# Turning softmax probabilities as rounded-kind data after a copy inside SBUF, in a one-core hybrid encoder layer

## The chip, the core and the metric

The program runs on one core of a Trainium2 chip. The metric is the device time of one execution in microseconds (us); the lower the better. Five engines work side by side, each through its own instruction stream in order: TensorE (PE, with a separate record PEld for the loading of the stationary operand), VectorE (DVE), ScalarE (ACT), GpSimd (POOL) and SyncE (SP). In this kernel SP issues nearly all DMA transfers. A stream that waits for a semaphore holds up everything behind it on the same engine.

## The reference

One encoder layer is applied to two token groups (1024 and 256 rows of width 2048, here 10 tiles of 128 rows). Everything is fp32. Cut to the lines that matter here:

```
hn = rms_norm(x, norm_g);  proj = hn @ w_in               # 2048 -> 4896 columns
o_ssd = chunked two-way state-space scan over xbc, dt     # 16 heads
# window attention, 8 heads of 64, 2 key heads, |t-s| <= 128, sink logit:
s = q @ k.T * 64**-0.5 - slope * dist                     # masked to the band
m = max(max(s), sink);  pr = exp(s - m)
probs = pr / (sum(pr) + exp(sink - m));  o_att = (probs @ v) * silu(z_att)
# memory attention, 4 heads of 128 against 256 memory rows:
pm = softmax(mq @ mk.T * 128**-0.5);  o_mem = (pm @ mv) * silu(z_mem)
y = x + concat[o_ssd, o_att, o_mem] @ w_out
```

For `probs @ v` and `pm @ mv` the tensor engine contracts over the partition axis, so the probabilities, which come out with queries on partitions, have to be turned to have keys on partitions.

## The kernel before, in words

The large products (`x @ w_in`, `mem @ w_mem_kv`, `o @ w_out`) are the trunk. Each weight block is loaded by SP into a `wraw` tile (pool of `RB = 4`), split by ACT and DVE into a high and a low part of the rounded fp32 kind (`wsplit`, L202 and L203, `fp32r`, pools of 3), and multiplied in three passes (L254 to L256 for token tiles, L289 to L291 for feature tiles, L1199 to L1201 for the seven-product blocks). The fp32r kind streams a 512-column product in about 0.23 us on this core; a plain fp32 product of the same width shows as two records of about 0.43 us each.

Beside the trunk run two lanes, which are queues of Python generators. Lane 0 holds `k_prep`, `attn` and `mem_attn`, tile after tile; lane 1 holds the state-space work `ssd_up` and `ssd_down`. After each step of a trunk block `run` calls `pump(rates)`: each lane is owed its rate (a number of generator steps; `RATES` has one pair, lane 0 and lane 1, for each weight block of each of the two row groups), and each step owed runs the generator to its next `yield`. So a `yield` is a unit of distance, and the rate says how many such units go to one trunk step.

The program is written in a tile framework. What the Python emits is a list in priority order; a planner then lays it out, engine by engine, with its own durations: at each point an engine takes the earliest instruction of the list whose inputs the planner holds to be ready and whose buffers are free. Slots of a pool tag are given out when the first writer of a tile is placed. The order that results is fixed in the program; on the chip each engine follows it and waits where an input is late.

`attn(t)` (one tile of 128 queries) loads `q`, normalises it, turns it in two halves (`pq`, L616, as fp32r with the fp32r identity `identr`), and loads the gate `za`. Then it goes over four head pairs `rr`: `scores(rr)` makes two score products into PSUM (`psc`, L632 and L633), DVE adds the distance bias into `lg` (L634, pool of 2), reduces the maximum, ACT takes the exponentials (L647), DVE scales by the reciprocal sum (L652, tile `lg<-lg,den`). `turn_(rr)` turns the probabilities as plain fp32 with `ident` (`ppt`, L664: two key heads times 2 or 3 blocks of 128) and ACT copies them out (`pT`, L665). `values(half)` multiplies two turned head pairs with `v` (`po`, L674) and DVE applies the gate into `oT` (L677). `mem_attn(t)` does the same over two head pairs `hp` with four blocks each: `pms` (L737 to L739), `mpr` (L746, L751), `pmt` (L759, fp32, `ident`), `mpT` (L763), `pmo` (L774).

The tag `wa` (pool of `WA = 5` slots of 128x512 fp32) holds `q`, its squares, the split `qh`, `za`/`zm`, `oT`/`moT` and small helpers of the lane. The functions that the change touches, with their lines:

Of the kernel before, what the change touches and what calls it, by code (L numbers as in the profile page):

```python
# [10 lines left out]
F32 = mybir.dt.float32  # L11
F32R = mybir.dt.float32r
# [7 lines left out]
P = 128  # L20
# [8 lines left out]
CH, WB, RB, WA, WBB = 4, 3, 4, 5, 4  # L29
RBB = 3  # L30

RATES = ({'kv': (2.0, 1.0), 'mq': (2.4, 1.6), 'z0': (2.2, 1.7), 'z1': (2.2, 1.7)},
         {'kv': (1.2, 1.5), 'x': (1.75, 1.85), 'q': (1.6, 2.5), 'za': (1.6, 2.5), 'z0': (1.55, 2.6),
          'z1': (1.55, 2.65), 'mq': (1.55, 2.8), 'zm': (1.55, 2.85), 'o': (1.95, 1.9)})
NEG = -1e30

UNITS = (0, 4, 1, 5, 2, 6, 7, 3, 8, 9)
# [6 lines left out]
def hymba_encoder_kernel(  # L44
# [42 lines left out]
    ident = identr.bitcast(F32)  # L87
# [495 lines left out]
    def attn(t):  # L583
        lo, hi = (0, NS) if t < NS else (NS, NT)
        k0, k1 = max(lo, t - 1), min(hi, t + 2)
        na = k1 - k0
        nk = na * P
        d0 = (k0 - (t - 1)) * P
        s0 = k0 if t < 4 else k0 - 3
        grp, ti = divmod(t, 5)  # L590
        tc_ = slice(ti * P, (ti + 1) * P)
        q = w2("q")
        S.dma_start(q, q_d[t])
        yield
        sq = w2("sq")
        A.activation(sq, q, AF.Square)
        ss = sm.tile([P, 8], F32, tag="s8", name="qss", bufs=4)
        V.reduce_sum(out=ss, in_=hv(sq), axis=AX.X)  # L598
        r = sm.tile([P, 8], F32, tag="s8", name="qr", bufs=4)
        rsqrt(r, ss, 1.0 / 64, 8)  # L600
        for _ in range(3):
            yield
        q3 = hv(q)
        V.tensor_mul(q3, q3, hb(r, 8, 64))
        yield
        qT = []
        for b in range(2):
            qh = mp.tile([P, 4, 2, 64], F32R, tag="wa", name="qh", bufs=WA)
            qb = q3[:, 4 * b:4 * b + 4, :]
            A.activation(qh[:, :, 0, :], qb, AF.Copy)  # L610
            V.tensor_sub(qh[:, :, 1, :], qb, qh[:, :, 0, :].bitcast(F32))
            yield
            ps = psum("pq")
            qf = qh.rearrange("p a b d -> p (a b d)")
            for a in range(4):
                T.transpose(ps[:, a * P:(a + 1) * P].bitcast(F32R), qf[:, a * P:(a + 1) * P], identr)  # L616
            o = mp.tile([P, 512], F32R, tag="qT", name="qT", bufs=2)
            A.activation(o, ps, AF.Copy)
            qT.append(o)
        z = w2("za")  # L620
        S.dma_start(hv(z, 4), zT_d[0][grp][:, :, tc_])
        yield
        sk8 = sinkb.rearrange("p (v r) -> p r v", v=2)
        state_ = {}

        def scores(rr):
            lg = mp.tile([P, 2, 384], F32, tag="lg", name="lg", bufs=2)
            for kv in range(2):
                h = 4 * kv + rr
                ps = psum("psc")  # L630
                st = qT[kv][:, rr * P:(rr + 1) * P]
                T.matmul(ps[:, :nk], st, kT[:, kv, s0 * P:s0 * P + nk], start=True, stop=False)  # L632
                T.matmul(ps[:, :nk], st, kL[:, kv, s0 * P:s0 * P + nk], start=False, stop=True)  # L633
                V.scalar_tensor_tensor(out=lg[:, kv, :nk], in0=ndist[:, d0:d0 + nk], scalar=2.0 ** -(h + 1),  # L634
                                       in1=ps[:, :nk], op0=ALU.mult, op1=ALU.add)
            m = sm.tile([P, 2], F32, tag="m2", name="m", bufs=10)
            V.reduce_max(out=m, in_=lg[:, :, :nk], axis=AX.X)
            sk = sk8[:, rr, :]
            nm = sm.tile([P, 2], F32, tag="m2", name="nm", bufs=10)
            V.tensor_max(m, m, sk)  # L640
            V.tensor_scalar(out=nm, in0=m, scalar1=-1.0, scalar2=None, op0=ALU.mult)
            es = sm.tile([P, 2], F32, tag="m2", name="es", bufs=10)
            V.tensor_add(es, sk, nm)
            A.activation(es, es, AF.Exp)
            den = sm.tile([P, 2], F32, tag="m2", name="den", bufs=10)
            for kv in range(2):
                A.activation(lg[:, kv, :nk], lg[:, kv, :nk], AF.Exp, bias=nm[:, kv:kv + 1],  # L647
                             accum_out=den[:, kv:kv + 1])
            V.tensor_add(den, den, es)
            V.reciprocal(out=den, in_=den)  # L650
            for kv in range(2):
                V.tensor_scalar(out=lg[:, kv, :nk], in0=lg[:, kv, :nk], scalar1=den[:, kv:kv + 1], scalar2=0.5,  # L652
                                op0=ALU.mult, op1=ALU.mult)
            state_[rr] = lg

        def turn_(rr):
            lg = state_.pop(rr)
            if rr % 2 == 0:
                state_["pT"] = mp.tile([P, 2, 2, 384], F32, tag="pT", name="pT", bufs=1)
            pT = state_["pT"]  # L660
            for kv in range(2):
                pt = psum("ppt")
                for a in range(na):
                    T.transpose(pt[:, a * P:(a + 1) * P], lg[:, kv, a * P:(a + 1) * P], ident)  # L664
                A.activation(pT[:, kv, rr % 2, :nk], pt[:, :nk], AF.Copy)  # L665

        oT = w2("oT")

        def values(half):
            pT = state_.pop("pT")  # L670
            po = psum("po")
            for a in range(na):
                for kv in range(2):
                    T.matmul(hv(po[kv * 64:kv * 64 + 64, :2 * P], 2), v_all[:, s0 + a, kv * 64:kv * 64 + 64],  # L674
                             pT[:, kv, :, a * P:(a + 1) * P], start=(a == 0), stop=(a == na - 1))
            c = slice(half * 2 * P, (half + 1) * 2 * P)
            V.tensor_mul(oT[:, c], po[:, :2 * P], z[:, c])  # L677

        scores(0)
        yield  # L680
        scores(1)
        yield
        yield
        turn_(0)
        yield
        scores(2)
        yield
        turn_(1)
        yield
        scores(3)  # L690
        yield
        values(0)
        yield
        turn_(2)
        yield
        turn_(3)
        yield
        yield
        values(1)
        yield  # L700
        S.dma_start(oT_d[0][grp][:, :, tc_], hv(oT, 4))


    def mem_attn(t):
# [26 lines left out]
        def scores(hp):  # L731
            ps = psum("pms")
            for j in range(2):
                h = 2 * hp + j
                c = slice(h * P, (h + 1) * P)
                o = ps[:, j * 256:(j + 1) * 256]
                T.matmul(o, qh[:, c], mkH[:, h, :], start=True, stop=False)  # L737
                T.matmul(o, qh[:, c], mkL[:, h, :], start=False, stop=False)
                T.matmul(o, ql[:, c], mkH[:, h, :], start=False, stop=True)  # L739
            m = sm.tile([P, 2], F32, tag="m2", name="mm", bufs=10)  # L740
            V.reduce_max(out=m, in_=hv(ps, 2), axis=AX.X)
            V.scalar_tensor_tensor(out=m, in0=m, scalar=-1.0, in1=r[:, 2 * hp:2 * hp + 2], op0=ALU.mult, op1=ALU.mult)
            pr = mp.tile([P, 512], F32, tag="lg", name="mpr", bufs=2)
            den = sm.tile([P, 2], F32, tag="m2", name="mden", bufs=10)
            for j in range(2):
                A.activation(pr[:, j * 256:(j + 1) * 256], ps[:, j * 256:(j + 1) * 256], AF.Exp,  # L746
                             scale=r[:, 2 * hp + j:2 * hp + j + 1], bias=m[:, j:j + 1], accum_out=den[:, j:j + 1])
            V.reciprocal(out=den, in_=den)
            for j in range(2):
                c = slice(j * 256, (j + 1) * 256)  # L750
                V.tensor_scalar(out=pr[:, c], in0=pr[:, c], scalar1=den[:, j:j + 1], scalar2=0.5,  # L751
                                op0=ALU.mult, op1=ALU.mult)
            st_[hp] = pr

        def turn_(hp):
            pr = st_[hp]
            pt = psum("pmt")
            for a in range(4):
                T.transpose(pt[:, a * P:(a + 1) * P], pr[:, a * P:(a + 1) * P], ident)  # L759
            if hp == 0:  # L760
                st_["pT"] = mp.tile([P, 2, 768], F32, tag="pT", name="mpT", bufs=1)
            pT = st_["pT"][:, hp, :512]
            A.activation(pT, pt, AF.Copy)  # L763
            st_[hp] = pT
# [13 lines left out]

        scores(0)
        yield  # L780
        scores(1)
        yield
        yield
        turn_(0)
        yield
        turn_(1)
        yield
        values(0)
        yield
        values(1)  # L790
        S.dma_start(oT_d[1][grp][:, :, tc_], hv(oT, 4))
# [889 lines left out]
```

## Time and profile before

| | |
|---|---|
| device time, median of 3 runs | 1804.51 us (1804.37 to 1805.38) |
| profiled execution, first to last instruction (span) | 1800.7 us |
| what the median has beyond that span | 3.8 us |
| PE busy | 1791.2 us, 99% of the span |
| DVE / ACT / POOL busy | 1244.3 / 903.0 / 439.5 us |
| granted TensorE clock | 1.000 over the span |
| DMA packets' share of the 16 engines | 52.7% |

The profile gives no separate device time for the profiled execution beside its span; the three runs agree within 1.0 us, and what lies around the span is taken to be the same in each. Durations of PE records overlap, because matmuls are pipelined: what a matmul costs is the distance from its start to the start of the next, not its recorded length. Waits name the engine and the tile that ended them.

### The profile page before, as it was taken

To read this page: it belongs to the slowest core of one execution; us is meant where nothing else is said; L and a number is where in the kernel's file an instruction comes from. 1 tells how busy PE (TensorE), PEld (TensorE's weight loads), DVE (VectorE), ACT (ScalarE), POOL (GpSimd) and SP (SyncE) were. 2 spreads that over 40 slices of the span, in tenths; PEclk is the share of its full clock that TensorE was granted. 3 is DMA by queue.
4 is the path that set the end of the run, shared out by engine and by line. 5 is a ranking of instruction groups with operands and counts; after the bars stand their busy time and mean duration, and the time that the engine had idled before them with its cause. 6 is when DMAs were issued, how large, how long until landed. Compare 5 with 4: busy or idle time off the path is not lost.

```text
span 1800.7 us, 30423 instructions
## 1 busy us (share of the span) xinstructions
PE 1791.2 (99%) x10546; PEld 1606.1 (89%) x10546; DVE 1244.3 (69%) x2422; ACT 903.0 (50%) x2039; POOL 439.5 (24%) x714
## 2 busy tenths in 40 slices
PE   9999999999999999999999999999999999999999
PEld 7789999999887899999989987887898888889999
DVE  5595788877657978775755866666885654866665
ACT  6554455444445756564435646544574533543332
POOL 0105789961110000000000000001100000058775
PEclk9999999999999999999999999999999999999999
DMA  8664455446544644444436355457785564644442
GB/s 291 198 179 120 138 153 146 129 136 218 164 136 147 184 134 140 121 132 134 119 96 192 110 161 180 128 178 235 231 266 168 184 190 138 216 153 147 142 143 80
DMA packets 198891, 290.58 MB, mean 161 GB/s; under 512 B 18960, under 2 KB 80464, under 8 KB 198736
## 3 DMA queue, kind: packets, MB, share of 16 engines
q1 hardware_dynamic: 198592, 288.57, 52.7%
q8 instruction: 83, 1.36, 0.3%
q14 instruction: 72, 0.59, 0.1%
q10 hardware_dynamic: 144, 0.06, 0.0%
HBM read 231.12 MB, written 57.44 MB: 160 GB/s over the span
## 4 chain that ended last, share of the span: by engine, by line
PE 61%; DVE 1%; ACT 1%; issue 1%; DMA 1%; POOL 0%; POOLq 0%; ACTq 0%; DVEq 0%
PE acc L254 9%; PE acc L256 8%; PE acc L255 8%; PE acc L289 5%; PE acc L291 5%; PE acc L290 5%; PE acc L1199 3%; PE acc L1201 3%; PE acc L1200 3%; PE py L931 2%; PE po L674 1%; PE ppt L664 1%; PE accm L1200 1%; PE accm L1201 1%; PE accm L1199 1%
## 5 line engine op out<-in xcount | busy, mean ns | idle before, releaser
L203 DVE TENSOR_TENSOR wl<-wraw,wh 128x512 fp32r<-128x512 f32 (+1 forms) x480 | 338.9, 708 | 241.3 <-ACT wh L202 230.7
L254 PE MATMUL acc<-wh,xH 128*128 128x512 f32 (+1 forms) x1248 | 481.9, 386 | 0.2 <-ACT mkr L416 0.2
L255 PE MATMUL acc<-wl,xH 128*128 128x512 f32 (+1 forms) x1248 | 472.2, 378 | 0.9 <-DVE wl L203 0.6
L256 PE MATMUL acc<-wh,xL 128*128 128x512 f32 (+1 forms) x1248 | 472.8, 379 | 0.0
L202 ACT ACTIVATE wh<-wraw 128x512 fp32r<-128x512 f32 (+1 forms) x480 | 292.4, 613 | 323.5 <-PE acc L256 173.3
L254 PEld LDWEIGHTS acc<-wh,xH 128*128 128x128 f32 x1248 | 234.5, 188 | 45.1 <-issue 4.8
L255 PEld LDWEIGHTS acc<-wl,xH 128*128 128x128 f32 x1248 | 234.7, 188 | 43.8 <-DVE wl L203 3.3
L256 PEld LDWEIGHTS acc<-wh,xL 128*128 128x128 f32 x1248 | 234.2, 188 | 43.9 <-issue 0.9
L289 PE MATMUL acc<-xH,wh 128*128 128x320 f32 x640 | 204.5, 320 | 0.0
L291 PE MATMUL acc<-xH,wl 128*128 128x320 f32 x640 | 198.6, 310 | 0.0
L290 PE MATMUL acc<-xL,wh 128*128 128x320 f32 x640 | 198.3, 310 | 0.0
L203 DVE TENSOR_TENSOR sl<-ws,sh 128x384 fp32r<-128x384 f32 x144 | 99.6, 695 | 96.9 <-ACT sh L202 96.6
L202 ACT ACTIVATE sh<-ws 128x384 fp32r<-128x384 f32 x144 | 74.6, 523 | 176.5 <-POOL ws L1171 81.5
L1171 POOL TENSOR_TENSOR ws<-wraw 128x128 f32<-128x128 f32 x144 | 91.1, 633 | 202.0 <-DMA wraw<-in_w_in_pairs_dram 83.6
L289 PEld LDWEIGHTS acc<-xH,wh 128*128 128x128 f32 x640 | 120.3, 188 | 4.1 <-issue 3.7
L290 PEld LDWEIGHTS acc<-xL,wh 128*128 128x128 f32 x640 | 120.3, 188 | 2.6 <-issue 2.2
L291 PEld LDWEIGHTS acc<-xH,wl 128*128 128x128 f32 x640 | 120.1, 188 | 0.7 <-issue 0.6
L1171 POOL TENSOR_TENSOR ws<-wraw,ws 128x128 f32<-128x128 f32 x144 | 93.5, 649 | 11.3
L358 DVE SCALAR_TENSOR_TENSOR c<-u,vec,c 128x638 f32<-128x638 f32 (+1 forms) x96 | 88.6, 926 | 10.0 <-ACT c L353 9.7
L1171 POOL TENSOR_TENSOR ws<-ws,wraw 128x128 f32<-128x128 f32 x144 | 94.2, 654 | 0.0
L120 POOL TENSOR_SCALAR qr<-qss 128x8 f32<-128x8 f32 x10 | 4.3, 428 | 366.6 <-DVE qss L598 366.6
L1171 POOL TENSOR_TENSOR wraw<-wraw 128x128 f32<-128x128 f32 x144 | 89.2, 620 | 11.1
(427 smaller groups left out, 3645.1 us busy)
## 6 DMA issues: line engine op xcount, KB each, us to landing
wraw<-in_w_in_laid_dram SPq DMA_DIRECT2D x208, 256.0 KB, 2.8
wraw<-in_w_in_pairs_dram SPq DMA_DIRECT2D x80, 256.0 KB, 2.8
wraw<-in_w_out_laid_dram SPq DMA_DIRECT2D x64, 256.0 KB, 3.5
wraw<-in_w_out_pairs_dram SPq DMA_DIRECT2D x64, 256.0 KB, 2.8
rf<-ac SPq DMA_DIRECT2D x40, 256.0 KB, 3.7
rb<-ac SPq DMA_DIRECT2D x40, 256.0 KB, 4.1
wraw<-in_w_mem_laid_dram SPq DMA_DIRECT2D x32, 256.0 KB, 4.8
xst<-in_x_sample_dram SPq DMA_DIRECT2D x20, 256.0 KB, 4.7
```

The costliest lines, as they stand in the source:

```text
L202: a = A.activation(h, raw, AF.Copy)
L203: b = V.tensor_sub(l, raw, h.bitcast(F32))
L254: T.matmul(ps[t][:, :n], sh, h[:, :n], start=(k_ == 0), stop=False)
L255: T.matmul(ps[t][:, :n], sh, l[:, :n], start=False, stop=False)
L256: T.matmul(ps[t][:, :n], sl, h[:, :n], start=False, stop=(k_ == KT - 1))
L289: T.matmul(o, sh, cur["H", q][:, m, c], start=(k == 0), stop=False)
L290: T.matmul(o, sh, cur["L", q][:, m, c], start=False, stop=False)
L291: T.matmul(o, sl, cur["H", q][:, m, c], start=False, stop=(k == KT - 1))
L358: V.scalar_tensor_tensor(out=c[0], in0=u[:, k:k + n], scalar=cw[k], in1=c[0], op0=ALU.mult, op1=ALU.add)
L1171: G.tensor_tensor(out=o, in0=x, in1=y, op=op)
L1199: T.matmul(ps[p], h, xh, start=(k_ == 0), stop=False)
L1200: T.matmul(ps[p], h, xl, start=False, stop=False)
```

## The change

- In `attn`, each scaled `lg` (two key heads) is copied by two SP transfers from SBUF to SBUF into two new tiles `lgR` of the fp32r kind, 128x384, in the tag `wa`. `turn_` turns `lgR` with `identr`, as fp32r.
- In `mem_attn`, `mpr` is copied by one SP transfer into `mprR` (128x512, fp32r, tag `wa`) and turned in the same way.
- The yields move: `attn` has 12 instead of 11 of them from its first scores to its last values, and four between `scores(rr)` and `turn_(rr)` for every head pair (before three or four). `scores(2)` now follows `turn_(0)` and `scores(3)` follows `turn_(1)` in the same step. `mem_attn` has 8 instead of 6, and four instead of three between the scores and the turn of each head pair; `values(0)` now comes before `turn_(1)`.
- The lane 0 entries of `RATES` are multiplied by about 1.07. Lane 1's are kept.

The transfers copy bits through an fp32 view of the destination; no value is changed by them.

```diff
--- before.py
+++ after.py
@@ -29,9 +29,8 @@
 CH, WB, RB, WA, WBB = 4, 3, 4, 5, 4
 RBB = 3
 
-RATES = ({'kv': (2.0, 1.0), 'mq': (2.4, 1.6), 'z0': (2.2, 1.7), 'z1': (2.2, 1.7)},
-         {'kv': (1.2, 1.5), 'x': (1.75, 1.85), 'q': (1.6, 2.5), 'za': (1.6, 2.5), 'z0': (1.55, 2.6),
-          'z1': (1.55, 2.65), 'mq': (1.55, 2.8), 'zm': (1.55, 2.85), 'o': (1.95, 1.9)})
+RATES = ({'kv': (2.14, 1.0), 'mq': (2.57, 1.6), 'z0': (2.35, 1.7), 'z1': (2.35, 1.7)},
+         {'kv': (1.28, 1.5), 'x': (1.87, 1.85), 'q': (1.71, 2.5), 'za': (1.71, 2.5), 'z0': (1.66, 2.6), 'z1': (1.66, 2.65), 'mq': (1.66, 2.8), 'zm': (1.66, 2.85), 'o': (2.09, 1.9)})
 NEG = -1e30
 
 UNITS = (0, 4, 1, 5, 2, 6, 7, 3, 8, 9)
@@ -651,7 +650,9 @@
             for kv in range(2):
                 V.tensor_scalar(out=lg[:, kv, :nk], in0=lg[:, kv, :nk], scalar1=den[:, kv:kv + 1], scalar2=0.5,
                                 op0=ALU.mult, op1=ALU.mult)
-            state_[rr] = lg
+            state_[rr] = [mp.tile([P, 384], F32R, tag="wa", name="lgR", bufs=WA) for _ in range(2)]
+            for kv in range(2):
+                S.dma_start(state_[rr][kv].bitcast(F32)[:, :nk], lg[:, kv, :nk])
 
         def turn_(rr):
             lg = state_.pop(rr)
@@ -661,7 +662,7 @@
             for kv in range(2):
                 pt = psum("ppt")
                 for a in range(na):
-                    T.transpose(pt[:, a * P:(a + 1) * P], lg[:, kv, a * P:(a + 1) * P], ident)
+                    T.transpose(pt[:, a * P:(a + 1) * P].bitcast(F32R), lg[kv][:, a * P:(a + 1) * P], identr)
                 A.activation(pT[:, kv, rr % 2, :nk], pt[:, :nk], AF.Copy)
 
         oT = w2("oT")
@@ -678,20 +679,21 @@
 
         scores(0)
         yield
+        yield
         scores(1)
         yield
         yield
         turn_(0)
-        yield
         scores(2)
         yield
+        yield
         turn_(1)
-        yield
         scores(3)
         yield
         values(0)
         yield
         turn_(2)
+        yield
         yield
         turn_(3)
         yield
@@ -750,13 +752,14 @@
                 c = slice(j * 256, (j + 1) * 256)
                 V.tensor_scalar(out=pr[:, c], in0=pr[:, c], scalar1=den[:, j:j + 1], scalar2=0.5,
                                 op0=ALU.mult, op1=ALU.mult)
-            st_[hp] = pr
+            st_[hp] = mp.tile([P, 512], F32R, tag="wa", name="mprR", bufs=WA)
+            S.dma_start(st_[hp].bitcast(F32), pr)
 
         def turn_(hp):
             pr = st_[hp]
             pt = psum("pmt")
             for a in range(4):
-                T.transpose(pt[:, a * P:(a + 1) * P], pr[:, a * P:(a + 1) * P], ident)
+                T.transpose(pt[:, a * P:(a + 1) * P].bitcast(F32R), pr[:, a * P:(a + 1) * P], identr)
             if hp == 0:
                 st_["pT"] = mp.tile([P, 2, 768], F32, tag="pT", name="mpT", bufs=1)
             pT = st_["pT"][:, hp, :512]
@@ -778,14 +781,16 @@
 
         scores(0)
         yield
+        yield
         scores(1)
         yield
         yield
         turn_(0)
         yield
+        values(0)
+        yield
         turn_(1)
         yield
-        values(0)
         yield
         values(1)
         S.dma_start(oT_d[1][grp][:, :, tc_], hv(oT, 4))
```

## The prediction

> **What bounds the kernel now.** I read the page's first two parts, then the waits of the tensor engine, then the groups of the turned tiles, then the timeline around them.
>
> ```profile
> span 1800.7 us, 30423 instructions
> PE 1791.2 (99%) x10546; PEld 1606.1 (89%) x10546; DVE 1244.3 (69%) x2422; ACT 903.0 (50%) x2039; POOL 439.5 (24%) x714
> PEclk9999999999999999999999999999999999999999
> q1 hardware_dynamic: 198592, 288.57, 52.7%
> ```
>
> PE is busy for 99% of the span at a granted clock that never drops. The waits of PE and of its weight loads, by what ended them (total us, times, longest):
>
> ```profile
> PE pmt L759 <- DVE mpr L751: 1.3, 2, 0.8
> PE ppt L664 <- DVE lg L652: 0.9, 2, 0.5
> PE acc L255 <- DVE wl L203: 0.6, 3, 0.2
> ...
> PEld acc L255 <- DVE wl L203: 3.3, 7, 0.5
> ```
>
> Nothing on PE waits for long: the weights cost it 3.9 us in all, the probabilities 2.2 us as matmul waits. So the bound is the sum of PE's own slots. Two rules follow for the whole estimate: PE time removed comes off the end one for one, and a wait put in front of a PE instruction is added one for one, because nothing else can overtake it there. Work on DVE, ACT and SP counts only when it makes PE wait.
>
> **The turning transposes.** These are the plain fp32 ones of both attentions (to be replaced) and the fp32r ones of the query (the kind that replaces them):
>
> ```profile
> L664 PE MATMUL ppt<-identr,lg x208: 270/272/329, 565.5 to 1349.4; 128*128 128x128 f32 x104
> L759 PE MATMUL pmt<-identr,mpr x80: 270/272/303, 767.1 to 1498.4; 128*128 128x128 f32 x80
> L616 PE MATMUL pq<-identr,qh x80: 220/248/260, 552.5 to 1317.0; 128*128 128x128 f32 x80
> ```
>
> There are 208 + 80 = 288 to replace. The recorded lengths (272 and 248 ns) include the pipeline; the cost is the slot. In the timeline of PE:
>
> ```profile
> 565.26 0.39 PE L256 MATMUL acc<-wh,xL 128*128 128x512 f32 x1
> 565.49 0.60 PE L664 MATMUL ppt<-identr,lg 128*128 128x128 f32 x4
> 565.84 0.48 PE L254 MATMUL acc<-wh,xH 128*128 128x512 f32 x1
> 566.16 0.40 PE L255 MATMUL acc<-wl,xH 128*128 128x512 f32 x1
> ...
> 552.50 0.80 PE L616 MATMUL pq<-identr,qh 128*128 128x128 f32 x8
> 553.13 0.47 PE L254 MATMUL acc<-wh,xH 128*128 128x512 f32 x1
> 553.44 0.40 PE L255 MATMUL acc<-wl,xH 128*128 128x512 f32 x1
> ```
>
> A 512-column product has a slot of 0.23 us (565.26 to 565.49). Four fp32 transposes and one such product take 566.16 - 565.49 = 0.67 us, so a transpose takes (0.67 - 0.23)/4 = 110 ns. Eight fp32r ones take (553.44 - 552.50 - 0.23)/8 = 89 ns. The difference is 21 ns, or 288 x 21 = 6.0 us. The chain of waits splits the hand-over to the next product in another way:
>
> ```profile
> 615.65 0.66 PE ppt L664 x6
> ...
> 706.58 0.63 PE pq L616 x8
> ```
>
> That is 110 against 79 ns, 31 ns apart and 8.9 us in all. I take 6.5 us, nearer to the first, which has the hand-over in it; 6.0 and 8.9 are the ends. ACT copies the same PSUM tiles out as before, so nothing else changes there.
>
> **The copy, which stands in the chain.** A turn now waits for scores, softmax, scaling, and then a transfer. In the trace the chain begins and ends like this (count; first and last start):
>
> ```profile
> L632 PE MATMUL psc<-kT,qT x80: 277/336/739, 557.2 to 1338.5; 128*128 128x384 f32 x48, 128*128 128x256 f32 x32
> L652 DVE TENSOR_SCALAR lg<-lg,den x80: 343/412/435, 564.5 to 1348.8; 128x384 f32<-128x384 f32 x48, 128x256 f32<-128x256 f32 x32
> L737 PE MATMUL pms<-mkH,mqh x40: 277/280/384, 757.0 to 1490.4; 128*128 128x256 f32 x40
> L751 DVE TENSOR_SCALAR mpr<-mpr,mden x40: 345/349/355, 761.8 to 1494.7; 128x256 f32<-128x256 f32 x40
> ```
>
> The first chain of attention runs from 557.2 to about 564.8 (7.6 us), the last from 1338.3 to 1349.1 (10.8 us); over the 40 head pairs, taken one by one, the mean is 8.6 us. For the memory heads the first is 5.1 us and the mean of 20 is also 5.1 us.
>
> Next, how much PE work the program puts over that chain. I laid the order of each built program out with the slots above, and summed the slots from the first score product to the first turn. Attention: 10.7 us before, 11.5 us after. Memory: 7.0 before, 9.5 after. The chain itself gets shorter, because the scores of two head pairs stand further apart: DVE's work in its own order between the first bias addition and the last scaling, summed with the durations of before, is 8.7 us before and 7.6 us after. So attention's room behind the scaling is 10.7 - 8.6 = 2.1 us before and 11.5 - 7.5 = 4.0 us after, a gain of 1.9 us. Memory: 7.0 - 5.1 = 1.9 and 9.5 - 5.1 = 4.4 us, a gain of 2.5 us.
>
> That gain is to be paid for the transfer. The trace has no copy from SBUF to SBUF. The nearest rows by size, and their neighbours (KB each, median us from issue to landing):
>
> ```profile
> wraw<-in_w_in_laid_dram SPq DMA_DIRECT2D x208, 256.0 KB, 2.8
> q<-qs SPq DMA_DIRECT2D x10, 256.0 KB, 3.2
> mq<-qs SPq DMA_DIRECT2D x10, 256.0 KB, 2.6
> xbc_d<-u SPq DMA_DIRECT2D x12, 193.0 KB, 2.2
> xbc_d<-u SPq DMA_DIRECT2D x12, 128.0 KB, 2.2
> ```
>
> Attention's copies are of 192 KB (six tiles) or 128 KB (four), memory's of 256 KB. I bound the wait at 2.2 and 3.2 us. I take 2.35 us for attention, nearest to the two rows of its sizes plus a little for the issue, and 2.7 us for memory, between 2.6 and 2.8. [...]
>
> The mean room is larger than the transfer, so only the turns that stand close behind their chain matter. Before, 18 of 40 in attention and 7 of 20 in memory start less than about 0.8 us behind the scaling. The last of attention is the clearest:
>
> ```profile
> 1348.21 0.39 PE L255 MATMUL acc<-wl,xH 128*128 128x512 f32 x1
> 1349.06 0.63 PE L664 MATMUL ppt<-identr,lg 128*128 128x128 f32 x4 [0.46 <-DVE lg L652]
> ```
>
> The planner does this: it puts a turn in as soon as it holds its input to be there. The 18 have 0.39 us to spare on average, memory's 7 about 0.35. Shifted by the gain in room less the transfer, each of the 18 is late by 2.35 - 1.9 - 0.39 = 0.06 us, in all 1.1 us; memory's are not late (2.7 - 2.5 - 0.35 < 0). Transfers scatter, and the late ones cost while the early ones give nothing: 1.4 us more is my allowance for it, about as much again as the mean gives. So the new waits come to 2.5 us. At 2.2 us they are 0; at 3.2 us they are 18 x 0.91 + 7 x 0.35 = 19 us, or about half of that if the next chain goes on while PE waits. The 2.2 us that PE waits for probabilities already are of the same sort, and I leave them in the sum as they are.
>
> **What the other parts cost.** SP issues 100 more transfers (80 + 20). An issue takes this long on SP, and SP already waits for the weights' buffers often and long:
>
> ```profile
> L368 SPq DMA_DIRECT2D xbc_d<-u x12: 319/326/382, 684.7 to 910.9; - x12
> ...
> SPq L209 <- DVE wl L203: 322.5, 148, 8.8
> ```
>
> 100 x 0.33 = 33 us over some 800 us of SP time. A copy waits on SP for the scaling, and what stands behind it are weight loads and other tiles; but SP has waited up to 8.8 us here and the weights still cost PE 3.9 us in the whole run. I put this at nothing; the cover is the four `wraw` buffers. Without it, each copy that holds up a weight load by 1 us would cost up to 1 us. 17 MB more on 290 MB moves the DMA share by 3 points of 53: nothing. The 10 yields more in attention and 20 in memory are matched by the 1.07 on lane 0; lane 0's last value product comes within 2 us of where it was in the laid-out order. Lane 1 keeps its rates. In `wa`, four `lgR` and `za` fill all five slots, so `oT` and the next `q` come later; they wait on SP and DVE, with a step or more in hand: nothing, or below 1 us. `lg` is now freed by the copy's landing, earlier than by the turn: nothing.
>
> **Sum.** Against the profiled span: 1800.7 - 6.5 + 2.5 = 1796.7. The median of the runs is 3.8 us above the span, which the change doesn't touch: 1800.5 us, 4.0 us or 0.22% less than 1804.5.
>
> **Rivals.**
> - *The copy lands late (slower).* The place is the weight load or the matmul of `ppt`, behind the copy. At 3.0 us, the mean of the two slower 256 KB rows, 18 x 0.71 + 7 x 0.15 = 14 us of waits, 7 to 14 with the overlap: 1805 to 1812, about 1809; at 3.2 us up to 1817. It decides from 1.9 + 0.39 + 6.5/18 = 2.65 us on, where the waits eat the gain. For it: 52.7% DMA share, so transfers queue behind 256 KB loads. Against it: the rows of 2.2 us.
> - *The waits eat the gain (no change).* Copies at 2.45 to 2.75 us, waits of 4 to 9 us: 1802 to 1807, about 1804.
> - *SP is held up and weights are late (slower).* If one copy in five delayed a split by 1 us: 20 us, 1818. Against it stands the 8.8 us row.
> - *The kind doesn't matter (slower).* If a turn's slot stays at 110 ns, because the operands come from another place than the query's: only the waits are left, 1804.5 + 2.5 = 1807, or 1808 and above with any scatter. The 89 ns come from the same identity and the same size, which speaks against it.
>
> **How the numbers follow.** About 0.2% (3.6 us) is what a measurement of this kernel can tell from no change. Chances: the forecast 0.41 (1797 to 1801); waits eat the gain 0.25; late copies 0.26; SP 0.04; kind 0.04. So faster 0.41, same 0.25, slower 0.34. Time 1800.5. The range leaves out one in ten on each side: low 1797.0, which is 6.5 us with hardly a wait and a bit more; high 1815.0, between the 1812 and the 1817 of the late copies. The forecast's own range is 1797 to 1801.
>
> **What would show it.** The turns' slots in the timeline near 89 ns, and PE busy in matmuls down by about 6 us: the gain. Waits of PE or its weight loads for the DMA `lgR<-lg` below 3 us in total: the room holds. Landing times of that transfer near 2.3 us. Weights' waits on PE unchanged near 4 us: SP holds nobody up. The prediction falls if PE waits for `lgR` or `mprR` add up to more than 6 us, or if the copies land after 2.6 us in the median.

## The result, and the profile after

| device time, us | median | range | runs |
|---|---|---|---|
| before | 1804.44 | 1802.66 to 1805.38 | 4 |
| changed | 1813.13 | 1810.00 to 1813.89 | 4 |

The changed kernel takes 1.0050 times as long as the one before (95% interval 1.0035 to 1.0064). It is 0.5% slower, some 9 us, where 0.2% faster was forecast. The profiled execution of the changed kernel took 1812.86 us around a span of 1811.2 us, so 1.7 us lie outside the span, not 3.8. With 1.7 us around it, the span of 1800.7 us shown before would be a run of about 1802.4 us, next to the fastest of the four runs of before, 1802.66 us, and not the median. That moves the forecast's base by 2 us and explains nothing of the loss.

The first two parts and the DMA groups of the changed kernel's page, in the order in which the prediction showed those of before (the DMA rows: KB each, median us from issue to landing):

```profile
span 1811.2 us, 30747 instructions
PE 1794.1 (99%) x10546; PEld 1603.3 (89%) x10546; DVE 1247.9 (69%) x2422; ACT 901.9 (50%) x2039; POOL 438.9 (24%) x714
PEclk9999999999999999999999999999999999999999
q1 hardware_dynamic: 212992, 307.45, 55.1%
...
wraw<-in_w_in_laid_dram SPq DMA_DIRECT2D x208, 256.0 KB, 2.9
...
lgR<-lg SPq DMA_DIRECT2D x48, 192.0 KB, 2.2
```

Nothing stands out here. PE is still busy for 99%, the DMA share rose by 2.4 points where 3 were forecast (the copies moved 18.9 MB, not 17), the large copies land after 2.2 us in the median, and the weights' loads take 2.9 instead of 2.8. PE busy rose by 2.9 us although the turns got cheaper. The answer for the copies' own tile says more (min/median/max; the first two rows are durations in ns, the last is us from issue to landing):

```profile
L665 PE MATMUL ppt<-identr,lgR x208: 221/245/627, 555.9 to 1359.5; 128*128 128x128 f32 x104
L655 SPq DMA_DIRECT2D lgR<-lg x80: 464/482/1169, 553.4 to 1354.8; - x80
...
DMA to landing us min/median/max: 1.9/2.4/6.2
```

The turns' records shrink from 272 to 245 ns. Measured from start to next start, summed over all 288, PE's slots in turns fell by 5.9 us (3.07 in attention, 2.87 in memory; median slot 109 to 82 ns). But that count leaves out the hand-over, which lengthens the slot of the product behind each run of turns, and the changed order has 84 such runs where before has 63. Counted with it, as in the prediction's first reading, four memory turns in a row cost 437 ns before and 370 ns after, and the sum over all 288 falls from 34.1 to 29.5 us, by 4.6 us. The gain is there, about 2 us smaller than forecast. But a copy can take 6.2 us, two and a half times the median. The waits of PE and its weight loads, by what ended them (total us, times, longest):

```profile
PE ppt L665 <- DMA lgR<-lg: 5.8, 7, 2.5
PEld ppt L665 <- issue: 5.6, 8, 2.9
PEld acc L254 <- DVE wl L202: 3.0, 7, 0.5
PE psc L631 <- DVE state L901: 1.3, 1, 1.3
PE pmo L777 <- ACT mpT L766: 1.1, 1, 1.1
```

Seven turns wait for copies, the weights wait as before, and waits appear that name neither copies nor turns. The largest wait lies in the first row group's attention. There SP's timeline and the DMA groups of the same 5 us show what the copy stood among:

```profile
604.49 0.33 SPq L208 DMA_DIRECT2D wraw<-in_w_in_laid_dram  x1
604.88 0.42 SPq L183 DMA_DIRECT2D chd<-in_x_turned_dram  x1
605.75 0.33 SPq L847 DMA_DIRECT2D rf<-ac  x1
606.52 0.33 SPq L183 DMA_DIRECT2D chd<-in_x_turned_dram  x1
607.41 1.11 SPq L655 DMA_DIRECT2D lgR<-lg  x2
```

```profile
q1 hardware_dynamic: 779, 1.41, 88.4%
...
chd<-in_x_turned_dram SPq DMA_DIRECT2D x3, 320.0 KB, 6.2
lgR<-lg SPq DMA_DIRECT2D x3, 192.0 KB, 5.7
wraw<-in_w_in_laid_dram SPq DMA_DIRECT2D x1, 256.0 KB, 3.6
rf<-ac SPq DMA_DIRECT2D x1, 256.0 KB, 6.2
```

From 603 to 608 us the DMA engines are 88% busy. Two of the copy's three neighbours are as late as the copy: `chd` and `rf` take 6.2 us, where their medians over the program are 3.4 and 3.8. The weight load takes 3.6 instead of 2.9. PE's timeline right behind it, and a table of stretches (us from the start; PE busy, PEclk and the DMA share are the columns to read):

```profile
610.47 0.39 PE L253 MATMUL acc<-wh,xH 128*128 128x512 f32 x1
613.32 0.42 PE L665 MATMUL ppt<-identr,lgR 128*128 128x128 f32 x3 [2.46 <-DMA lgR<-lg]
...
615.56 2.74 PE L675 MATMUL po<-pT,v_all 128*64 128x256 f32 x12
```

```profile
603.00:615.00 12.00, 9.54 (x50) 7.65 (x49) 9.54 (x22) 7.44 (x22) 0.00 (x0) 0.99 0.80 251
615.00:618.20 3.20, 3.20 (x14) 1.35 (x13) 2.98 (x7) 1.30 (x6) 0.00 (x0) 0.52 0.01 2
618.20:640.00 21.80, 21.80 (x115) 17.39 (x114) 17.62 (x35) 13.46 (x33) 1.83 (x2) 1.00 0.73 229
```

The wait costs 2.5 us. Then the granted clock falls to half for 3.4 us (0.50 from 614.67 to 618.09 us). The twelve `po` products take 2.74 us in it, and 1.51 us at the full clock from 682.24 us on. By estimate, half of the 3.4 us, the products in it take about 1.7 us longer. The digits of the page's clock line hide this, because one slice is 45 us long.

Against the trunk's products of before, matched one by one, the changed kernel is 1.1 us late at 480 us (before any turn), 9.7 us at 627 us, and 9.9 us at the end. In between, lane work that comes earlier or later moves it up and down. So the net loss arises in the first attention stretch. Later losses are balanced by what the turns give.

### The profile page after: what moved, and what is told of

Same layout as the page of the kernel before. It is cut to its first block, busy times and chain, and to the rows that moved or that the text cites. A ratio compares the mean times of both kernels' runs of the same rounds, so it can differ in the third digit from the quotient of the medians.

```text
span 1811.2 us, 30747 instructions
## 1 busy us (share of the span) xinstructions
PE 1794.1 (99%) x10546; PEld 1603.3 (89%) x10546; DVE 1247.9 (69%) x2422; ACT 901.9 (50%) x2039; POOL 438.9 (24%) x714
## 3 DMA queue, kind: packets, MB, share of 16 engines
q1 hardware_dynamic: 212992, 307.45, 55.1%
```

## The experiments

Each kernel ran beside the kernel before on the same chip. Ratios are to before, with 95% intervals; 0.1% is 1.8 us. The theories at the start, as the expectations number them: (1) the loss is PE waiting for copies that land late; (2) the new order of steps costs it; (3) the copies cost through what they take from others (SP, the DMA engines, the `wa` slots), whoever reads them.

**The order alone.** The new yields and rates, the turns of before, no copies:

```diff
-            state_[rr] = [mp.tile([P, 384], F32R, tag="wa", name="lgR", bufs=WA) for _ in range(2)]
-            for kv in range(2):
-                S.dma_start(state_[rr][kv].bitcast(F32)[:, :nk], lg[:, kv, :nk])
+            state_[rr] = lg
...
-                    T.transpose(pt[:, a * P:(a + 1) * P].bitcast(F32R), lg[kv][:, a * P:(a + 1) * P], identr)
+                    T.transpose(pt[:, a * P:(a + 1) * P], lg[:, kv, a * P:(a + 1) * P], ident)
```

> Only the yields and the rates of the change; the probabilities are turned as plain fp32 straight from lg and mpr, with no transfer. Theory 1 (the loss is PE waiting for copies that land late): within 2 us of the kernel before, 1803 to 1806, no group of waits on PE above 3 us. Theory 2 (the new order of steps costs it): 1810 to 1815. Theory 3 (the copies load SP, the DMA engines and the wa slots, whoever waits): 1803 to 1806, as theory 1.

1804.64 us beside 1802.55, ratio 1.0011 (1.0002 to 1.0020). The new order costs 2.0 us by itself, and theory 2 is not the main loss.

**The copies without a reader.** As above, and the 100 copies are made into `wa` tiles that nobody reads:

```diff
+            for kv in range(2):
+                cp_ = mp.tile([P, 384], F32, tag="wa", name="lgR", bufs=WA)
+                S.dma_start(cp_[:, :nk], lg[:, kv, :nk])
```

> The yields, the rates and all 100 transfers into wa tiles as in the change, but nobody reads the copies: the turns are plain fp32 from lg and mpr. Theory 1: 1803 to 1807. Theory 2: 1810 to 1815. Theory 3: 1809 or more, with waits on PE for weights or other loads up by 4 us or more.

1811.87 us, ratio 1.0051 (1.0038 to 1.0064): as much as the changed kernel loses, with no turn waiting for a copy and no gain from the turns. Theory 1 alone is out, and theory 3 gets the time right, though not its sign: PE does not wait more for weights. Of this kernel, a late stretch on ACT and PE:

```profile
1351.59 0.82 ACT L195 ACTIVATE xH<-chd,vec 128x640 fp32r<-128x640 f32 x1
1355.38 0.83 ACT L195 ACTIVATE xH<-chd,vec 128x640 fp32r<-128x640 f32 x1 [2.97 <-DMA chd<-oT]
1356.11 0.36 ACT L667 ACTIVATE pT<-ppt 128x256 f32<-128x256 f32 x1
...
1356.53 0.50 PE L863 MATMUL pst<-fh,bth 128*128 128x512 f32 x1 [2.67 <-ACT pT L667]
```

```profile
1330.00:1345.00 15.00, 14.93 (x107) 14.04 (x107) 14.02 (x38) 12.48 (x38) 0.00 (x0) 1.00 0.96 305
1345.00:1360.00 15.00, 12.33 (x60) 8.58 (x57) 10.97 (x24) 11.87 (x32) 0.00 (x0) 0.92 0.83 278
```

A trunk load (`chd`) lands late, ACT waits for it with the copy-out of an old turn queued behind, and the state-space product that follows on PE waits for that. Nobody named in the chain is a copy. The order alone has no such hole here, though its DMA share in the two stretches is 0.91 and 0.86, about as high. So a busy DMA is not enough for it.

The two kernels lose alike in total but not in the same places. Matched product by product, this one is 5.3 us late at 627 us, where the changed kernel is 9.7, and loses 5.3 us more between 1345 and 1360 us, where the changed kernel loses 2.1.

**The copies from ACT's queue.** The changed kernel, with `A.dma_start` for `S.dma_start`:

> The change as it is, but the 100 copies are issued from ACT's queue and not from SP's. Theory 1, with the late landings caused by loads ahead in the same queue: the longest landing falls from 6 us to below 4, PE waits for lgR below 2 us, the clock is not halved, 1800 to 1805. Theory 2: 1810 to 1815. Theory 3: 1807 to 1813, since the DMA engines carry the same bytes and ACT pays 0.5 us for each issue.

1834.44 us, ratio 1.0172 (1.0154 to 1.0191). PE's waits for copies grow from 5.8 to 21.3 us:

```profile
PE ppt L665 <- DMA lgR<-lg: 21.3, 17, 4.0
```

The slowest copy lands after 6.9 us, no sooner than in SP's queue. So it is not the loads ahead of it in its own queue that make it late; theory 1 falls in that form.

**The rounding by DVE, no copies.** The order of before; the last scaling writes the rounded-kind tiles itself, so the probabilities are rounded there:

```diff
+            state_[rr] = [mp.tile([P, 384], F32R, tag="wa", name="lgR", bufs=WA) for _ in range(2)]
             for kv in range(2):
-                V.tensor_scalar(out=lg[:, kv, :nk], in0=lg[:, kv, :nk], scalar1=den[:, kv:kv + 1], scalar2=0.5,
+                V.tensor_scalar(out=state_[rr][kv][:, :nk], in0=lg[:, kv, :nk], scalar1=den[:, kv:kv + 1], scalar2=0.5,
                                 op0=ALU.mult, op1=ALU.mult)
-            state_[rr] = lg
```

> The kernel before with its own yields and rates; the last scaling on DVE writes the probabilities into fp32r tiles of the tag wa, so they are rounded there, and the turn is fp32r with identr: no transfer at all. This leaves the full precision of the probabilities out. Theory 1: the turns save 6 us and nothing waits for a copy: 1797 to 1800. Theory 2: the same. If a turn's slot doesn't matter to the end: 1803 to 1806.

1799.31 us, ratio 0.9982 (0.9973 to 0.9991). It is faster than both kernels. Of the 0.26% that the turns' 4.6 us would give, 0.18% came (the 5.9 us of the narrower count would be 0.33%).

**The same in the new order.** As before, with the change's yields and rates:

> The changed kernel with its yields and rates, but without transfers: DVE's last scaling writes the rounded-kind tiles itself (the probabilities are rounded there), and the turns are of the rounded kind. If the transfers alone spoil the change, this is 1804.6 less 5.9, 1797.5 to 1800.5, 11 to 15 us below the changed kernel. If the new order of steps is worse than the old one by 2 us in every setting, it is 1 to 3 us above the same edit in the old order (1799.3). If rounded turns make the order itself late, it is above 1802.

1799.66 us beside 1801.09, ratio 0.9991 (0.9983 to 1.0000): 0.09 points above the kernel in the old order, as the order alone cost 0.11. So taking the transfers out of the change is worth 0.6 points, about 11 us.

**The kind of the turn.** The changed kernel; the copies are turned as plain fp32 (`lgR`, `mprR` as F32, `ident` for `identr`):

> The changed kernel with its copies, waits and yields, but plain fp32 turns of the copy. If the turn's kind is worth the 5.9 us that the slots show, this is 5 to 7 us above the changed kernel: 1817 to 1820 beside 1811 to 1814. If the gain is eaten by waits that grow because PE arrives earlier, it is within 2 us of the changed kernel.

1815.49 us beside 1801.09, ratio 1.0076 (1.0063 to 1.0089). That is 0.26 points above the changed kernel, 4.7 us, close to the 4.6 us that the slots show with the hand-over, though the two intervals alone would allow 1 to 8 us.

**Copies with a sixteenth of the bytes, and copies of a constant.** Both are the kernel whose copies nobody reads; the first cuts each copy's columns by 16, the second reads the constant `mkH`, so that SP waits for no scaling and `lg` isn't held:

```diff
-                S.dma_start(cp_[:, :nk], lg[:, kv, :nk])
+                S.dma_start(cp_[:, :nk // 16], lg[:, kv, :nk // 16])
```

```diff
-                S.dma_start(cp_[:, :nk], lg[:, kv, :nk])
+                S.dma_start(cp_[:, :nk], mkH.bitcast(F32).rearrange("p a b -> p (a b)")[:, :nk])
```

> The 100 copies that nobody reads (1811.9 us, 7 us above the same order without copies, 1804.6), each cut to a sixteenth of its columns: the same waits of SP for the scaling, the same issues and slots, almost the same order, but 1 MB in place of 17 MB. Theory A, the bytes on the DMA engines make all transfers late in crowded stretches: 5 to 7 us go away, 1805 to 1807. Theory B, SP waits for the scaling in front of each pair of copies (about 100 us in all in the changed kernel, up to 5.9 at once) and the loads queued behind come late: nothing goes away, 1810 to 1813. A mixture would lie at 1808 to 1809.

> The other half of the pair: the same 100 unread copies with all their bytes, but reading a constant tile in place of the scaled probabilities, so SP waits for no scaling there and lg is held by no transfer. The order differs a little on PE and more on SP. Theory A (bytes): 1810 to 1813. Theory B (SP's waits for the scaling): 1804.5 to 1807, and SP's waits for lg and mpr in front of copies gone from about 100 us to below 20.

The first: 1809.69 us, ratio 1.0040 (1.0027 to 1.0053). The second: 1806.73 us, ratio 1.0028 (1.0018 to 1.0038). Without the bytes most of the loss stays, so the bytes' share is about 0.1 points. Without the wait for the scaling and without the hold on `lg`, more than half goes away (0.40 to 0.17 points above the order alone). That looked like SP, which stands in front of the copies while loads queue up behind it. But this kernel differs in a third way: its copies need nothing from the chain and come early, and the next tile's `q`, which shares the tag `wa`, is loaded at 561.0 us, against 570.7 us in the kernel whose copies are full and unread. Its waits there are long in the changed kernel:

```profile
SPq L655 <- DVE lg L651: 67.5, 30, 5.9
SPq L756 <- DVE mpr L753: 33.2, 15, 3.7
```

**The copies from GpSimd's queue, without and with a reader.** `G.dma_start` for `S.dma_start`, in the kernel whose copies nobody reads and in the changed kernel:

> The 100 full copies that nobody reads, issued from GpSimd's queue in place of SP's (in SP's queue they cost 0.40% over the same order without copies, 0.51 against 0.11% above the kernel before). If it is SP's waiting for the scaling with the loads queued behind it (about 4 us of the 7), this gives back 3 to 5 us: 0.2 to 0.35% above before. If the lateness comes from the bytes and the held lg tile, it stays at 0.45 to 0.55%. GpSimd can lose: it waits for the same scalings, and the state-space lane's work is behind it; then above 0.6%.

> The changed kernel, its copies issued from GpSimd's queue and read by the rounded turns. If SP's queue is the main loss, 0.1 to 0.3% above before in place of 0.5%. If the turns' waits for copies in crowded stretches are the main loss, 0.45 to 0.6%. If GpSimd holds up the state-space lane, above 0.8%, with waits of PE for POOL's tiles.

1818.78 us, ratio 1.0083 (1.0070 to 1.0097), and 1855.11 us, ratio 1.0279 (1.0265 to 1.0293). In the first, GpSimd waits in front of the copies

```profile
POOL lgR L656 <- DVE lg L651: 201.0, 25, 31.0
```

with the state-space lane's work behind it. So this does not test SP's part; it shows a worse place.

**The copies emitted later.** Three yields behind the scores, one in front of the turn:

```diff
         scores(1)
         yield
+        copy_(0)
         yield
         turn_(0)
         scores(2)
         yield
+        copy_(1)
         yield
         turn_(1)
```

`copy_` holds the two transfers that `scores` issued; the other pairs and `mem_attn` are moved in the same way.

> The changed kernel with each copy emitted three yields after its scores, one before its turn, so that SP reaches it later and waits less in front of it. Expected of theory B (SP's waits): SP's waits for lg and mpr in front of copies fall from about 100 us to below 50; the time falls by 1 to 4 us if the turns do not wait more, 0.3 to 0.45% above before. Rival: the copies land later, PE's waits for them grow from 6 us, and the time is 0.5 to 0.9% above before.

1810.95 us, ratio 1.0041 (1.0028 to 1.0053). SP's waits did not change:

```profile
SPq L659 <- DVE lg L651: 65.7, 29, 5.8
SPq L768 <- DVE mpr L761: 33.4, 15, 3.7
```

The planner puts a copy in when it holds the input to be ready, not where the program emits it. The kernel did not do what it was made for, and decides nothing.

**The memory attention alone.** New order, copies and rounded turns in `mem_attn` only:

> Yields and rates of the change; copy and rounded turn only in the memory attention (20 copies, 80 turns), attention plain fp32 without copies. Nearly all the drift of the changed kernel arises in attention's stretches, so this should be at the order's own cost less 80 x 26 ns = 2.1 us plus little: 1802.5 to 1804 on a scale where before is 1802.5, or -0.05 to +0.1%. If memory's copies lose as much for each copy as attention's (9 us for 100), it is +0.1 to +0.2%.

1803.49 us beside 1802.84, ratio 1.0002 (0.9993 to 1.0011): the order's 0.11 less about 0.09, or 1.6 us of the 2.1 expected. Memory's part is no loss. The loss is attention's.

**SP's issues and waits alone, and with `lg` held.** In place of each copy SP issues one of 128x2 values into a small tile of its own. The source is `den` in the first kernel, two columns of the scaled probabilities in the second:

```diff
-                S.dma_start(cp_[:, :nk], lg[:, kv, :nk])
+                S.dma_start(sm.tile([P, 2], F32, tag="cpx", name="lgR", bufs=4), den)
```

```diff
-                S.dma_start(cp_[:, :nk], lg[:, kv, :nk])
+                S.dma_start(sm.tile([P, 2], F32, tag="cpx", name="lgR", bufs=4), lg[:, kv, :2])
```

> The order of the change without real copies: in the place of each copy SP issues one of 128x2 values (the sums of the softmax, den) into a small tile of its own, which nobody reads. SP is issued as many transfers and waits for nearly the same point of the chain, but no lg, no wa slot and no bytes are held. If SP's issues and waits make up most of what unread copies cost (0.29 points above the same order without copies for the ones cut to a sixteenth), this is 0.30 to 0.45% above before. If what costs is that lg and wa are held until the copy lands, it is 0.05 to 0.2%.

> The same with two columns of the scaled probabilities as the source: SP waits for the scaling itself, and lg is held until the small copy lands; still no wa slot and nearly no bytes. SP theory: 0.30 to 0.45%, as the kernel with den. Holding lg: clearly above that one, 0.3 to 0.4 against 0.05 to 0.2%. Holding wa slots: both at 0.05 to 0.2%, and the copies cut to a sixteenth (0.40%) stand alone.

The first: 1803.36 us, ratio 1.0006 (0.9998 to 1.0015). The second: 1805.51 us, ratio 1.0015 (1.0005 to 1.0024). The waits of SP are there in the first,

```profile
SPq L655 <- DVE den L649: 70.6, 38, 4.9
```

and cost nothing that can be measured. The second kernel's SP waits for the scaling itself, as long as SP does in the kernel with a sixteenth of the bytes (46.7 and 35.2 us there):

```profile
SPq L655 <- DVE lg L651: 45.4, 30, 5.5
SPq L756 <- DVE mpr L753: 36.1, 17, 3.7
```

The theory of SP's waits by themselves falls. Holding `lg` adds 0.09 points, not told from nothing. Between the second kernel (0.15%) and the one with a sixteenth of the bytes (0.40%) the small copies move into `wa` tiles, and that step of 0.25 points, 4.5 us, stands outside the intervals. The planner also lays these two out in different orders, since it knows when the slots are free. Matched product by product, the one with `wa` tiles falls behind the other by 4.1 us between 480 and 627 us and by 2.8 us between 1345 and 1360 us. The second place is the hole shown above: the order with `wa` tiles puts the copy-out of the last attention turn behind the late `chd` on ACT, the other puts it in front. In the earlier stretch the next tile's `q` (tag `wa` too) is loaded 6 us later, and the second product of its scores waits; these rows are from the kernel without `wa` tiles, then from the one with them:

```profile
564.88 0.58 SPq L592 DMA_DIRECT2D q<-q  x1
...
592.41 0.44 PE L631 MATMUL psc<-kT,qT 128*128 128x384 f32 x1
```

```profile
571.18 0.58 SPq L592 DMA_DIRECT2D q<-q  x1
...
592.05 0.45 PE L631 MATMUL psc<-kT,qT 128*128 128x384 f32 x1 [1.01 <-ACT qT L617]
...
601.72 0.94 PE L666 MATMUL ppt<-identr,lg 128*128 128x128 f32 x6 [1.25 <-DVE lg L651]
```

**q in a slot of its own.** Four kernels: the changed one with `q` in its own tag and `wa` at 4 slots (the same memory); with `wa` at 5 and the lane's tag `wb` at 3; the control with `wb` at 3 alone; and the kernel without copies (old order, DVE rounds) with `q` in its own tag and `wa` at 4:

```diff
-        q = w2("q")
+        q = mp.tile([P, 512], F32, tag="qown", name="q", bufs=1)
```

> The changed kernel, with the next tile's q in a slot of its own in place of the tag wa, which has 4 slots for it instead of 5: the same memory. q's load no longer stands behind the previous tile's copies in SP's queue. If the wa slots that the copies hold cost by making the next q late (it was issued at 562 to 565 us in the orders without wa copies and at 570 to 572 us with them), 2 to 5 us come back: 0.2 to 0.4% above before in place of 0.5%, and q is issued before 566 us. Rival: qh, za and oT, which still share the tag and now have one slot less, wait instead, and the time stays or rises, 0.45 to 0.8%.

> The same with wa left at 5 slots, paid for by one slot of the state-space lane's tag (3 instead of 4). With both q free and wa not cut, the theory of the slots gives 0.15 to 0.35%; if the wa slots are not what costs, it equals the control with the lane's tag cut alone.

> The control: the changed kernel with the state-space lane's tag at 3 slots and nothing else. Its order is nearly that of the changed kernel: 0.45 to 0.6% above before, if the lane does not need the fourth slot.

> No transfers, old yields and rates, DVE's scaling writes the rounded tiles (probabilities rounded there), with q in a slot of its own and wa at 4. Without the slot it was 0.18% below before, of the 0.33% that the turns' 5.9 us would give. If late q took the rest, 0.2 to 0.35% below before; if the four wa slots now bind, 0.1% below to 0.1% above.

In this order: 1812.61 us, ratio 1.0058 (1.0045 to 1.0072); 1810.27 us, 1.0050 (1.0036 to 1.0064); 1807.52 us, 1.0039 (1.0026 to 1.0052); 1797.58 us beside 1801.96, 0.9979 (0.9970 to 0.9988). In the first there is no wait in the scores near 592 us (the kernel above waits 1.01 us for `qT` there; the changed kernel waits 1.30 us in the same scores, but for `state`),

```profile
591.24 0.44 PE L631 MATMUL psc<-kT,qT 128*128 128x384 f32 x1
...
595.36 0.34 PE L631 MATMUL psc<-kT,qT 128*128 128x384 f32 x1
```

and up to 627 us this execution loses 4 us less than the changed kernel. But it loses again where `qh` now has a slot less: near 1192.7 us the scores wait 0.80 us for `qT`, and half clock follows (0.51 from 1193.0 to 1196.5 us). The time did not fall, and the control lies lower than both. So the late `q` is one place where the slots bite, not the cause. The control, which should have changed nothing, moved by 0.11 points. The last kernel is the fastest measured here, 0.21% or 3.8 us below before, but it is not told from the 0.18% without the slot: the late `q` cost nothing there that can be measured.

A kernel already shown goes against the slots as such. Where DVE rounds in the new order, the same tiles lie in `wa`, held for 3.9 us in the median from the scaling to the last turn, and the next `q` is as late as with the copies:

```profile
569.48 0.33 SPq L592 DMA_DIRECT2D q<-q  x1
```

If tiles in `wa` cost 0.25 points wherever they stand, this kernel would be at 0.11 + 0.25 - 0.26 = 0.10% above before. It is 0.09% below (0.17 below to 0.00). It frees `lg` earlier, which may give some of that back. So a full tag and a late `q` are not enough for the 4.5 us. Whether the rest comes of a transfer that must wait for a slot in SP's queue, or only of the order that the planner happened to lay out, no run here separates.

## Why the prediction was wrong

The step that failed is the charge for the copies. The prediction let them cost time only through the turns that wait for them. All else that they do (SP's issues, the DMA share, `lg`, the slots of `wa`) it put at nothing, or below 1 us. The copies that nobody reads cost 0.40 points over the same order without copies, 7.2 us. What inside the copies costs that is only in part found.

In points of a percent, from the ratios above: the order 0.11; copies that nobody reads 0.40 more, of which SP's issues and waits are -0.05, the hold on `lg` 0.09, the `wa` tiles with the order they bring 0.25 and the bytes 0.11; reading the copies (changed kernel with plain turns less unread copies) 0.25; the rounded turns -0.26. Each is the difference of two neighbouring kernels, so they sum to 0.50 by construction; that they add up proves nothing, and unread and read copies lose in different places. The single steps of 0.05 to 0.11 are of the size by which a new layout alone moves the time.

- *The turns, -6.5 us.* Right in kind and too large: 4.6 us in PE's slots with the hand-over, 4.7 us in time.
- *The waits for copies, +2.5 us.* Too small: 4.5 us in time, 5.8 us of PE's waits in the trace. The medians were right (2.2 to 2.5 us against 2.35 and 2.7). What failed is the 1.4 us of allowance for scatter: the 18 copies of the changed kernel issued while the DMA share was 80% or more (from 1 us before the issue to 3 us behind it) took 2.6 to 6.2 us, 4.1 in the median, against 2.2 us for the 26 below 40%. The bounds of 2.2 and 3.2 came from medians. Taken alone, these two terms nearly cancel: that was the rival in which waits eat the gain.
- *SP's 100 issues, nothing.* Right in time, though an issue took 0.48 us and not 0.33, and SP waits 100 us in front of the copies.
- *The DMA share, nothing.* The share came out near the forecast, at 55.1%; the cost of the bytes, 0.11 points, isn't told from nothing.
- *The yields, matched by the rates.* Wrong by 2.0 us (0.4 to 3.6). The prediction had lane 0's last value product within 2 us of its old place; with the order alone it starts at 1512.1 us, 7.6 us later than before.
- *The slots of `wa`, "nothing, or below 1 us".* The largest step found inside the unread copies, 4.5 us, stands here. The prediction saw that `oT` and the next `q` come later and put them down as having a step in hand. They come later, 6 us for `q`. But the kernel in which DVE rounds has them late as well and does not lose, so this step is a difference of two laid-out programs and not a price of the slots alone. Its cause stays open.
- *The clock.* The prediction read it as full and held it fixed. In the profiled execution it was 0.50 for 3.4 us behind the wait of 2.46 us, by estimate about 1.7 us of time.
- *"A wait is added one for one."* Wrong for the longest one, for the same reason: behind 2.5 us of waiting came the half clock, some 1.7 us by the same estimate.

The rival of late copies (1805 to 1812 us) came nearest in time, but by another way: it asked for copies of 3.0 us in the median. The rival of SP and late weights asked for weights' waits, which stayed at about 4 us. No rival has the loss that the kernels show, without a reader and without late weights.

## What to carry to other kernels

To price a copy added to a tuned kernel, make a kernel with the copies that nobody reads: here it showed as large a loss as the change itself, before any turn waited. In a program that a planner lays out, test a new tile by itself; a new order alone moved the time by 0.1% here. Where the last engine to write a tile can write the kind that the next one wants, and rounding there is allowed, let it: here that gave 0.2% where the transfer lost 0.5%. Take the time of a transfer from the stretch in which it will run, not from a median over the program.

## What the runs showed of the hardware

**A small copy inside SBUF was little faster than a large one here.** From issue to landing (min/median/max us), copies of 1 KB in the kernel that issues `den`, then copies of 128 and 192 KB in the changed kernel:

```profile
DMA to landing us min/median/max: 1.6/1.8/5.0
```

```profile
DMA to landing us min/median/max: 1.9/2.4/6.2
```

The medians are 1.8 and 2.4 us. A copy of 1 KB could be late too, 5.0 us at the most. In the changed kernel the tail goes with the stretch: 4.1 us in the median for the 18 copies issued at a DMA share of 80% or more, counted as above, against 2.2 us for the 26 below 40%.

**In four traces half clock came behind short waits of PE.** In the changed kernel the wait of 2.46 us ended at 613.32 us, and the clock was 0.50 from 614.67 to 618.09 us. With the copies in ACT's queue, PE was busy for 0.87 of the 4.40 us up to 1382.4 us, and the clock was 0.50 in the 3.40 us behind. With `q` in a slot of its own and `wa` at 4, a wait of 0.80 us behind 1.96 us of products of 64 columns and four turns of the query ended at 1192.72 us, and the clock was 0.51 from 1193.0 to 1196.5 us; in that stretch a 512-column product has a slot of 0.43 us, where it has 0.23 us before. The kernel whose copies nobody reads, around its wait of 2.67 us (PE busy first, PEclk third from the end):

```profile
1353.40:1357.60 4.20, 1.53 (x7) 0.69 (x8) 1.45 (x3) 2.22 (x6) 0.00 (x0) 1.00 0.83 288
1357.60:1361.00 3.40, 3.40 (x12) 2.00 (x11) 2.44 (x6) 3.25 (x9) 0.00 (x0) 0.50 0.56 173
1361.00:1365.00 4.00, 4.00 (x19) 3.24 (x18) 2.87 (x5) 1.27 (x2) 2.30 (x2) 1.00 0.85 221
```

The length of the wait alone does not tell: behind the changed kernel's waits of 1.30, 1.22 and 1.05 us, which ended at 593.98, 1358.70 and 1382.07 us, the clock stayed at 1.00 for the next 5 us and more, while 0.80 us in the other kernel had half clock behind it.
